# Gated product of two halves: three 64 KiB input buffers, products packed over rows already read, one store per pair of tiles

## The chip, the core and the metric

The kernel runs on one core of one Trainium2 chip. The time is the device time of one execution in microseconds (us), the median of three runs. The profile shows one execution; its span, from the first to the last instruction that it records, is a little shorter than the run's time.

Four names are needed. ACT is the engine that computes activation functions, DVE the one that multiplies tensors; SP here only issues transfers. A transfer between main memory (DRAM) and the on-chip memory (SBUF, 128 partitions) is put on the queue of SP or of ACT, and 16 DMA engines carry it out. A queue is worked off in order.

## The reference

```python
def setup_inputs():
    batch, seq, dim = (32, 512, 2048)
    return {'x': np.random.randn(batch, seq, dim).astype(np.float32)}

def reference(x):
    half_dim = x.shape[-1] // 2
    x1, x2 = (x[..., :half_dim].copy(), x[..., half_dim:].copy())
    silu_x1 = x1 * (1 / (1 + np.exp(-x1)))
    return (silu_x1 * x2).astype(np.float32)
```

The input is 16,384 rows of 2,048 float32 values (134.22 MB), the output 16,384 rows of 1,024 (67.11 MB).

## The kernel before

The rows are cut into 16 tiles of 1,024 rows. A tile puts `K = 8` rows on each of the 128 partitions: 64 KiB of input and 32 KiB of output per partition. Two tiles that follow each other form a pair (`RUN = 2`): partition p holds 16 rows that are neighbours in DRAM, the first 8 in the pair's even tile, the other 8 in its odd one. So one load reads 64 KiB at a stretch for each partition, and one store writes 32 KiB at a stretch.

There are two input buffers `xt0`, `xt1` and two output buffers `ot0`, `ot1`, used in turn.

- `load(i)` (through `move`, line 77) puts the load of tile i on SP's queue. It waits until the tile two before has been multiplied, since that frees its buffer.
- `compute(i, ...)` applies silu in place to the first half of each row on ACT (line 96), then multiplies both halves into `ot` on DVE (line 102). A tile is one ACTIVATE and one multiply. The first tile is cut in four parts of 2 rows (`FIRST`), the last in parts of 2, 3 and 3 rows (`LAST`), so that DVE can start on a part while ACT works on the next.
- `store(i, ...)` (line 77 again) puts the store of tile i on ACT's queue, where it waits for the tile's multiplies. The first tile's store is cut in three by partitions (`OPENING`), the last tile's in three by rows.
- `settle_all_but(1, ...)` makes SP wait for every transfer but the last and for the last multiplies (line 67), ahead of the wait that ends the kernel.
- `implied` tells the framework that a dependency is covered by another, so that it adds no wait for it; `after` fixes the order in which transfers take their semaphores.

The order on ACT and DVE is the order of the program (`manual_schedule`). In the loop each tile is computed, then its store and the load of the tile after next are put on their queues.

Of the kernel before, what the change touches and what calls it, by code (L numbers as in the profile page):

```python
# [1 line left out]

# [4 lines left out]


@with_exitstack
def kernel(  # L10
    ctx: ExitStack,
    tc: tile.TileContext,
    x: bass.AP,
    out: bass.AP,
):


    nc = tc.nc
    P = nc.NUM_PARTITIONS

    x_flat = x.flatten_outer_dims()
    out_flat = out.flatten_outer_dims()
    num_rows, in_cols = x_flat.shape
    half = in_cols // 2
    dt = x_flat.dtype

    K = 8
    FIRST = [2] * (K // 2)
    LAST = [2, 3, 3]
    OPENING = [  # L30
        (slice(0, None, 4), slice(None)),
        (slice(2, None, 4), slice(None)),
        (slice(1, None, 2), slice(None)),
    ]
    RUN = 2
    n_tiles = num_rows // (P * K)

    pool = ctx.enter_context(tc.tile_pool(name="pool", bufs=1))
    xts = [pool.tile([P, K, in_cols], dt, name=f"xt{b}") for b in range(2)]
    ots = [pool.tile([P, K, half], dt, name=f"ot{b}") for b in range(2)]  # L40

    def view(flat, i):
        return flat.rearrange("(g p t k) d -> g t p k d", p=P, t=RUN, k=K)[i // RUN, i % RUN]

    ctx.enter_context(tc.manual_schedule(engines={mybir.EngineType.Activation, mybir.EngineType.DVE}))

    sent = []
    loads, stores, silus, muls = {}, {}, {}, {}

    def implied(later, earlier, reason):  # L50
        for x in later:
            for y in earlier:
                tc.declare_no_dep(x, y, reason=reason)

    def earlier(done, i):
        return [ins for j in range(i % 2, i, 2) for ins in done[j]]

    def after(later, first):
        tc.add_manual_dep(
            later,  # L60
            first.name,
            mybir.DependencyInfo(mybir.DependencyClass.NoSync, mybir.DependencyReason.DATA),
            reason="order in which the transfers take their semaphores",
        )

    def settle_all_but(n, others):
        rest = nc.sync.nop(nofuse=True)
        for ins in sent[:-n] + others:
            tc.add_manual_dep(
                rest.ins,  # L70
                ins.name,
                mybir.DependencyInfo(mybir.DependencyClass.Sync, mybir.DependencyReason.DATA),
                reason="sync sees each earlier transfer land before the last ones",
            )

    def move(queue, out, in_):
        ins = queue.dma_start(out=out, in_=in_).ins  # L77
        sent.append(ins)
        return ins

    def load(i):
        loads[i] = [move(nc.sync, xts[i % 2][:], view(x_flat, i))]
        if i >= 2:
            implied(loads[i], earlier(loads, i), "the multiplies that this load awaits came after those loads")
            implied(loads[i], earlier(silus, i), "the multiplies that this load awaits came after those activations")

    def parts(sizes):
        assert sum(sizes) == K
        return [slice(sum(sizes[:n]), sum(sizes[:n + 1])) for n in range(len(sizes))]

    def compute(i, ot, chunks):
        xt = xts[i % 2]
        silus[i], muls[i] = [], []
        for ks in chunks:
            silus[i].append(
                nc.scalar.activation(  # L96
                    out=xt[:, ks, :half],
                    in_=xt[:, ks, :half],
                    func=mybir.ActivationFunctionType.Silu,
                ).ins  # L100
            )
            muls[i].append(nc.vector.tensor_mul(out=ot[:, ks], in0=xt[:, ks, :half], in1=xt[:, ks, half:]).ins)  # L102
        implied(muls[i], loads[i], "each multiply awaits an activation that came after the load")
        if i >= 2:
            implied(silus[i], earlier(silus, i), "the load that this activation awaits came after those activations")
            implied(silus[i], earlier(muls, i), "the load that this activation awaits came after those multiplies")
            implied(muls[i], earlier(muls, i), "the store that this multiply awaits came after those multiplies")

    def store(i, ot, pieces):
        ov = view(out_flat, i)  # L110
        stores[i] = [move(nc.scalar, ov[ps, ks], ot[ps, ks]) for ps, ks in pieces]

    ALL = slice(None)
    load(0)
    load(1)
    for i in range(n_tiles):
        ot = ots[i % 2]
        last = i == n_tiles - 1
        compute(i, ot, parts(FIRST if i == 0 else LAST if last else [K]))
        pieces = [(ALL, ALL)]  # L120
        if i == 0:
            pieces = OPENING
        elif last:
            pieces = [(ALL, ks) for ks in parts(LAST)]
        load_first = i // 4 % 2
        if load_first and i + 2 < n_tiles:
            load(i + 2)
        store(i, ot, pieces)
        if load_first and i + 2 < n_tiles:
            after(stores[i][0], loads[i + 2][0])  # L130
        if not load_first and i + 2 < n_tiles:
            load(i + 2)
            after(loads[i + 2][0], stores[i][-1])
    settle_all_but(1, muls[n_tiles - 1])


# [1 line left out]
_INS = ['x']  # L138
_OUTS = [((32, 512, 1024), 'float32')]


# [23 lines left out]
```

## Time and profile before

| | |
|---|---|
| median of 3 runs | 470.94 us (470.73 to 471.01) |
| span of the profiled execution | 469.19 us |
| median less span | 1.75 us |
| bytes moved, mean rate over the span | 201.33 MB, 429 GB/s |
| loads | 16, median 42.2 us from issue to landing |
| stores of a whole tile | 14, median 42.0 us from issue to landing |
| ACTIVATE of a whole tile | 7029 ns |
| multiply of a whole tile | 8692 ns |
| ACTIVATE of 2 rows, of 3 rows | 1900 ns, 2747 ns |
| multiply of 2 rows, of 3 rows | 2288 ns, 3355 ns |

The profiled execution's time beyond its span is not recorded by itself; the table's third row stands for it. "q1" in the profile is SP's queue and holds the loads, "q10" is ACT's and holds the stores. "ACT" and "DVE" rows are work of an engine, "ACTq" and "SPq" rows are transfers being put on a queue, which take no time of the engine proper. The packet records of the trace, which the prediction uses too, give each contiguous run that a DMA engine moves its start, its length and its queue. In a row, "x4" counts instructions, and the bracket gives the time that the engine sat idle before it and what ended that.

### The profile page before, as it was taken

The numbers are of one execution on the slowest core, as the hardware profiler recorded it, in microseconds if no ns is written. First come the engines' busy times: TensorE is split into PE (matmuls) and PEld (weight loads), VectorE is DVE, ScalarE is ACT, GpSimd is POOL, SyncE is SP. The second block draws the span as 40 slices with busy tenths as digits, with TensorE's granted clock in tenths as the row PEclk, the third lists the DMA queues.
The fourth block names the chain that finished last, engine by engine and source line by source line (L and its number), as shares of the span: only waits on it lengthen the run. The fifth ranks groups of instructions, "written<-read, shape, count | busy, mean of one in ns | idle before, by whom it ended". The sixth has DMA issues, their size and how long they took to land.

```text
span 469.2 us, 156 instructions
## 1 busy us (share of the span) xinstructions
DVE 139.5 (30%) x21; ACT 114.2 (24%) x22; POOL 0.2 (0%) x4
## 2 busy tenths in 40 slices
DVE  0070522407034070330704307042070520605152
ACT  1051405032050410504105050050501405014060
POOL 0000000000000000000000000000000000000000
DMA  8999999999999999999999999999999999999998
GB/s 358 447 447 374 475 402 433 416 492 402 411 439 486 408 402 447 475 419 402 444 439 458 402 436 413 492 402 416 433 486 408 402 447 475 419 402 444 450 402 358
DMA packets 4928, 201.33 MB, mean 429 GB/s; under 512 B 576, under 2 KB 576, under 8 KB 576
## 3 DMA queue, kind: packets, MB, share of 16 engines
q1 hardware_dynamic: 2304, 134.22, 66.4%
q10 hardware_dynamic: 2624, 67.11, 33.2%
HBM read 134.22 MB, written 67.11 MB: 429 GB/s over the span
## 4 chain that ended last, share of the span: by engine, by line
DMA 72%; DVE 14%; ACT 11%; DVEq 1%; issue 0%; SPq 0%
DMA xt<-in_x_dram 72%; DVE ot L102 14%; ACT xt L96 11%; DVEq L160 1%; SPq L77 0%
## 5 line engine op out<-in xcount | busy, mean ns | idle before, releaser
L102 DVE TENSOR_TENSOR ot<-xt 128x8192 f32<-128x8192 f32 (+2 forms) x21 | 139.5, 6659 | 320.8 <-ACT xt L96 320.8
L96 ACT ACTIVATE xt<-xt 128x8192 f32<-128x8192 f32 (+2 forms) x21 | 112.9, 5400 | 341.4 <-DMA xt<-in_x_dram 341.4
L96 ACT ACT_TABLE_LOAD x1 | 1.3, 1283 | 0.7 <-PEq L149 0.7
L149 POOL MEMSET const-bfloat16-1.0<- 128x1 bf16 x1 | 0.1, 102 | 0.0
L149 POOL MEMSET const-uint8-127<- 128x1 uint8 x1 | 0.1, 102 | 0.0
L149 POOL MEMSET const-float32-0.0<- 128x1 f32 x1 | 0.1, 99 | 0.2 <-issue 0.2
L149 POOL MEMSET const-float32-1.0<- 128x1 f32 x1 | 0.1, 99 | 0.0
## 6 DMA issues: line engine op xcount, KB each, us to landing
out_dram<-ot ACTq DMA_DIRECT2D x14, 4096.0 KB, 42.0
out_dram<-ot ACTq DMA_DIRECT2D x3, 1024.0 KB, 12.0
out_dram<-ot ACTq DMA_DIRECT2D x2, 1536.0 KB, 7.9
out_dram<-ot ACTq DMA_DIRECT2D x1, 2048.0 KB, 37.2
xt<-in_x_dram SPq DMA_DIRECT2D x16, 42.2
```

The lines of the kernel that those rows point to most:

```text
L96: nc.scalar.activation(out=xt[:, ks, :half], in_=xt[:, ks, :half], func=mybir.ActivationFunctionType.Silu,).ins
L102: muls[i].append(nc.vector.tensor_mul(out=ot[:, ks], in0=xt[:, ks, :half], in1=xt[:, ks, half:]).ins)
L149: nc = _bacc.Bacc("TRN2", target_bir_lowering=False, num_devices=1)
L160: with _tile.TileContext(nc) as tc:
```

## The change

Three input buffers of 64 KiB per partition take the place of two input and two output buffers: `even0` and `even1` for the even tiles of alternate pairs, and `odd` for every odd tile. There is no output buffer. The products of a pair are written into the pair's even buffer, as 16 rows of 4 KiB: those of the even tile into its first 32 KiB, over input rows that have been read, those of the odd tile into the other 32 KiB. Each pair is then stored in one transfer, 64 KiB at a stretch per partition, 8 stores in all where there were 20.

Every even tile is computed in two parts of 4 rows (`EVEN`), every odd tile in parts of 2, 3 and 3 (`ODD`). Three loads are put on SP's queue at the start. The load of the next odd tile waits for the products of the present one; the load of the even tile two pairs on waits for the store of the present pair, which reads the same buffer. The store of the last pair but one is put on ACT's queue after the two activations of tile 14 instead of at the end of its own pair; the last pair's store is a single transfer, after all of tile 15. `OPENING`, `FIRST`, `settle_all_but`, `after` and the uses of `implied` go.

```diff
     K = 8
-    FIRST = [2] * (K // 2)
-    LAST = [2, 3, 3]
-    OPENING = [
...
     RUN = 2
+    EVEN = [4, 4]
+    ODD = [2, 3, 3]
     n_tiles = num_rows // (P * K)
+    n_pairs = n_tiles // RUN
...
-    xts = [pool.tile([P, K, in_cols], dt, name=f"xt{b}") for b in range(2)]
-    ots = [pool.tile([P, K, half], dt, name=f"ot{b}") for b in range(2)]
-
-    def view(flat, i):
-        return flat.rearrange("(g p t k) d -> g t p k d", p=P, t=RUN, k=K)[i // RUN, i % RUN]
+    evens = [pool.tile([P, K * in_cols], dt, name=f"even{b}") for b in range(2)]
+    odd = pool.tile([P, K * in_cols], dt, name="odd")
+
+    x_tiles = x_flat.rearrange("(g p t k) d -> g t p (k d)", p=P, t=RUN, k=K)
+    out_pairs = out_flat.rearrange("(g p r) d -> g p (r d)", p=P, r=RUN * K)
...
+    def home(i):
+        return odd if i % 2 else evens[i // 2 % 2]
...
+    def load(i):
+        loads[i] = [move(nc.sync, home(i)[:], x_tiles[i // 2, i % 2])]
+
+    def compute(i):
+        xt = home(i)[:].rearrange("p (k d) -> p k d", k=K)
+        products = evens[i // 2 % 2][:].rearrange("p (r d) -> p r d", r=RUN * K)
         silus[i], muls[i] = [], []
-        for ks in chunks:
+        for ks in parts(ODD if i % 2 else EVEN):
             silus[i].append(
...
+            rs = slice(i % 2 * K + ks.start, i % 2 * K + ks.stop)
+            muls[i].append(
+                nc.vector.tensor_mul(out=products[:, rs], in0=xt[:, ks, :half], in1=xt[:, ks, half:]).ins
+            )
...
+    def store(g):
+        stores[g] = [move(nc.scalar, out_pairs[g], evens[g % 2][:])]
...
-    settle_all_but(1, muls[n_tiles - 1])
+    for i in range(3):
+        load(i)
+    for g in range(n_pairs):
+        last = g == n_pairs - 1
+        compute(2 * g)
+        if last:
+            store(g - 1)
+        compute(2 * g + 1)
+        if g < n_pairs - 2 or last:
+            store(g)
+        if not last:
+            load(2 * g + 3)
+        if g + 2 < n_pairs:
+            load(2 * g + 4)
```

More of the change, by code (lines that the diff above doesn't have):

```diff
@@ L27 @@
     K = 8
-    FIRST = [2] * (K // 2)
-    LAST = [2, 3, 3]
-    OPENING = [
[L31 to L34, printed above, removed]
     RUN = 2
+    EVEN = [4, 4]
+    ODD = [2, 3, 3]
     n_tiles = num_rows // (P * K)
+    n_pairs = n_tiles // RUN
     pool = ctx.enter_context(tc.tile_pool(name="pool", bufs=1))
-    xts = [pool.tile([P, K, in_cols], dt, name=f"xt{b}") for b in range(2)]
-    ots = [pool.tile([P, K, half], dt, name=f"ot{b}") for b in range(2)]
-    def view(flat, i):
-        return flat.rearrange("(g p t k) d -> g t p k d", p=P, t=RUN, k=K)[i // RUN, i % RUN]
+    evens = [pool.tile([P, K * in_cols], dt, name=f"even{b}") for b in range(2)]
+    odd = pool.tile([P, K * in_cols], dt, name="odd")
+    x_tiles = x_flat.rearrange("(g p t k) d -> g t p (k d)", p=P, t=RUN, k=K)
+    out_pairs = out_flat.rearrange("(g p r) d -> g p (r d)", p=P, r=RUN * K)
     ctx.enter_context(tc.manual_schedule(engines={mybir.EngineType.Activation, mybir.EngineType.DVE}))
@@ L53, in implied @@
                 tc.declare_no_dep(x, y, reason=reason)
[L55 to L74, printed above, removed]
     def move(queue, out, in_):
@@ L79, in move @@
         return ins
[L81 to L85, printed above, removed]
     def parts(sizes):
@@ L89, in parts @@
         return [slice(sum(sizes[:n]), sum(sizes[:n + 1])) for n in range(len(sizes))]
-    def compute(i, ot, chunks):
-        xt = xts[i % 2]
+    def load(i):
[3 more added lines that the diff above has]
+        products = evens[i // 2 % 2][:].rearrange("p (r d) -> p r d", r=RUN * K)
         silus[i], muls[i] = [], []
-        for ks in chunks:
+        for ks in parts(ODD if i % 2 else EVEN):
             silus[i].append(
@@ L101, in compute @@
             )
[L102 to L133, printed above, removed]
-    settle_all_but(1, muls[n_tiles - 1])
+            rs = slice(i % 2 * K + ks.start, i % 2 * K + ks.stop)
[18 more added lines that the diff above has]
+            load(2 * g + 4)
 _INS = ['x']
```

## The prediction

> **What bounds the kernel now.** I read the page first, for the busy shares, the DMA rows and the chain.
>
> ```profile
> DVE 139.5 (30%) x21; ACT 114.2 (24%) x22; POOL 0.2 (0%) x4
> DMA  8999999999999999999999999999999999999998
> ...
> q1 hardware_dynamic: 2304, 134.22, 66.4%
> q10 hardware_dynamic: 2624, 67.11, 33.2%
> ```
>
> Both compute engines idle for over two thirds of the span. The loads (q1) and stores (q10) together fill 66.4 + 33.2 = 99.6% of the 16 DMA engines. So the bytes are the bound, and the change can win only what is left idle: start and end.
>
> Then the busy share by stretch (columns: stretch, length, DVE, ACT, POOL, clock, DMA share, GB/s), to find where that rest lies.
>
> ```profile
> 391.00:449.00 58.00, 17.39 (x2) 14.06 (x2) 0.00 (x0) 1.00 1.00 434
> 449.00:457.70 8.70, 6.32 (x3) 7.22 (x3) 0.00 (x0) 1.00 0.98 425
> 457.70:469.20 11.50, 2.60 (x1) 0.00 (x0) 0.00 (x0) 1.00 0.85 363
> ```
>
> A pair of tiles takes 58.0 us with DMA full. After the last load lands (449.06) DMA stays full too: the row at 449.00 is 98% busy on what is left of tile 14's store while tile 15 is computed. I call such work *cover*. The change rearranges just that cover.
>
> Next, the DMA view from 402 to 413 us, in slices of 0.275 us, each packet counted where it starts.
>
> ```profile
> GB/s 2145 1430 238 0 0 0 0 0 0 1430 357 119 0 1907 1668 238 0 0 0 0 0 0 1072 715 119 0 1192 1907 715 0 0 0 0 0 0 953 834 119 0 1192
> ```
>
> Groups of about 3,800 (loads) and 1,900 (stores) alternate: while both queues hold work, each DMA engine takes one run of a load, one of a store, and so on. From the trace's packet records: a 64 KiB run takes 2.418 us, a 32 KiB run 1.213, a 12 KiB run 0.460, and starts of 64 KiB runs are 2.4145 apart. A transfer over 128 partitions is 8 runs on each engine. The engines run up to 0.64 us apart, and a transfer is seen as landed 0.36 us after its last run.
>
> Last, the end in order of time (start, length, engine):
>
> ```profile
> 435.92 0.34 ACTq L77 DMA_DIRECT2D out_dram<-ot  x1
> 449.08 4.56 ACT L96 ACTIVATE xt<-xt 128x2048 f32<-128x2048 f32 x2 [21.91 <-DMA xt<-in_x_dram]
> 451.02 2.29 DVE L102 TENSOR_TENSOR ot<-xt 128x2048 f32<-128x2048 f32 x1 [15.13 <-ACT xt L96]
> 453.35 0.34 ACTq L77 DMA_DIRECT2D out_dram<-ot  x1
> 453.55 2.75 ACT L96 ACTIVATE xt<-xt 128x3072 f32<-128x3072 f32 x1
> 453.68 6.63 DVE L102 TENSOR_TENSOR ot<-xt 128x3072 f32<-128x3072 f32 x2 [0.36 <-ACT xt L96]
> ```
>
> Two readings matter. The last tile in rows 2, 3, 3 takes 449.08 to 460.30 = 11.22 us. And the store at 453.35 is issued while the second ACTIVATE runs (to 453.64) and before the third starts: an issue on ACT's queue does not wait for activations that are running or ready ahead of it. One that still waits for its data does hold the queue: a semaphore check for tile 3's store, long satisfied, is recorded at 101.09, just after that tile's ACTIVATE starts at 101.08.
>
> **The change, part by part.** *Packets.* Loads stay 128 runs of 64 KiB per engine. Stores were 120 runs of 32 KiB, 8 of 8 and 16 of 12 per engine: 120 x 1.213 + 8 x 0.309 + 16 x 0.460 = 155.4 us. They become 64 of 64 KiB; priced like a load's 2.418, 154.8. With the start-to-start figure and fewer completion packets I get -0.35 (bounds -0.7 and 0).
>
> *Start.* Three loads are queued at once, and the first store waits for tile 1, not tile 0. Load 1 lands at 22.66 + 8 x 2.4145 = 41.98, its products are done 11.22 later, at 53.2, with load 2 under way since 40.96. DMA is never without work: 0. The one-off 0.85 us by which a load's runs grow just before the first store's (starts 36.14 to 39.57 in before) moves along: 0.
>
> *Middle.* Load 4 and each later even one now waits for the store two pairs back to land, and stands in SP's queue; the odd load before it is issued already. Stores take every second slot. Store 0 is issued 12.3 us, or 5.1 runs, after load 2's first run. Before, the first store was issued at 33.53, during a load's run; one more load run went, then the store's. So here: 7 runs of load 2, then alternating. When store 0's 8th run ends, 2 runs of load 3 are left, 4.83 us. Load 4 needs 0.64 + 0.36 to see the landing and 1.0 from issue to first run (load 0: 0.73 to 1.73), in all 2.0. 2.8 us to spare, and each pair repeats this, since every phase hangs on the load ahead. The added waits on SP (0.02 to 0.05 us each) hide in it. Price 0. ACT's queue holds store g behind tile 2g+1's products; tile 2g+2's load lands 11 us later, so no activation is late. In-place products: DVE and ACT off the path except for tile 15, same 11.22.
>
> *End.* No store runs while load 14 finishes alone. Store 6 stands behind tile 14's two activations; the first waits for load 14, the second is ready behind it. By the 453.35 row the store is issued as soon as the first starts, 1.0 us after load 14's last run on the earliest engine, and ready 1.0 later, inside load 15's first run. One more load run follows, then they alternate. After load 15's 8th run, store 6 has had 6 runs; 2 remain, 4.83 us of cover. The last store's first run comes 1.0 (landing) + 0.02 + 11.22 (tile 15) + 0.03 + 1.0 (issue) = 13.27 us after load 15's end. DMA then idles 13.27 - 4.83 = **8.44 us**. One run later or earlier at the join gives 6.0 or 10.9.
>
> After that pause the first run may be longer: the only row of a run on idle engines is the first of the execution, 3.225 against 2.418, +0.8 for a load. No such growth shows on a store: +0.4, bounds 0 and 0.8. The last store is one piece, so its bytes no longer flow while the tile is computed; that is in the 8.44. Without the wait gathered on SP ahead of the end (15.69 us long in its record at 449.07, hidden), some checks may follow the last landing: +0.1, bounds 0 and 0.4.
>
> Sum: -0.35 + 8.44 + 0.4 + 0.1 = +8.6 us. On the profiled span of 469.19 that is 477.8; the median 470.94 is 1.75 more, for what lies around the span, so **479.5 us**.
>
> **A rule against a row.** The Trainium skill, "DMA: Bandwidth & Descriptors", section on queues, rings and completion order, says an engine drains a whole packet, typically 9 to 17 descriptors, from one ring before it takes the next. The view from 402 us shows the switch after every single run, so here the trace differs. The rule is rival 4's.
>
> **Rivals.**
> 1. *Not slower: store 6 is really held back.* If its issue comes after both activations have run (7029 ns for a whole tile by the page, so some 7.2 us for the two), it joins after load 15's 5th run, 5 runs of cover remain (12.07), idle is 1.2, and the time is 470.94 - 0.35 + 1.2 + 0.5 = 472.3; one run later it is nil, and the time 470.7 (without a pause, no first-run cost). It decides from an issue 6 us or more after load 14 lands. For it: the order written down. Against: the 453.35 row.
> 2. *Not held at all.* If the issue passes an activation that waits, store 6 goes at tile 13's end, is gone before load 15 lands, and nothing covers: +13.27, so 470.94 - 0.35 + 13.27 + 0.5 = 484.4. Against: the check at 101.09. The Trainium skill, "Perfetto Trace Analysis", on DVE and Act instructions, has the wait in a queue of the engine while the sequencer goes on; that would give this rival, and the 101.09 record speaks against it.
> 3. *The store's run is cut.* If 64 KiB goes as two of 32, store g has 16 slots, load 2g+3 ends with 7 still to go, and load 2g+4 starts 2.0 us late, six times; at the end 10 short runs (12.1) cover all but 1.2: 470.94 + 12 + 1.2 + 0.5 = 484.6. Against: loads of the same contiguous shape are single runs, 2048 packets of 64 KiB.
> 4. *Whole transfers alternate.* Then load 15 ends before store 6 starts, whose 19.3 us cover the 13.27: 470.94 - 0.35 + 0.1 = 470.7.
>
> **How the numbers follow.** Forecast 0.82: join as worked out 0.55, one run later (477.1) 0.2, one earlier (481.9) 0.07. Rivals: 0.07, 0.05, 0.03, 0.03. The lowest of the one-later case without its 0.5 is 476.6; the one-earlier case gives 482.0 rounded up. That range holds 0.82. A difference of 0.2% is 0.94 us, about what a measurement here can tell from none. Within it: rival 4 and half of rival 1, 0.06. Faster by more: no case, since only -0.35 is to be had; 0.02 for 64 KiB store runs faster than any row shows (6% would be needed even to undo the pause). Slower: the rest, 0.92.
>
> **What would show it.** Right: stores landing in about 39 us each, the last in about 20; DMA near 1.00 until some 4.8 us after the last load, then a hole of 8 us in its row; the held store issued within 0.2 us of tile 14's first ACTIVATE; last ACTIVATE group starting near 444. Wrong: that store issued 7 us after it (rival 1) or before it (2); holes all along (3); loads landing in 20 us beside a store (4).

## The result, and the profile after

The changed kernel takes 489.29 us (median of 5 runs, 487.93 to 490.69) against 470.94 us: a ratio of 1.039, 95% interval 1.037 to 1.041. The forecast was 479.5 us, range 476.6 to 482.0. The direction was right; the loss is twice as large: 18.35 us where 8.6 were worked out. The profiled execution has a span of 487.41 us (before: 469.19).

The page of the changed kernel, the same rows as before:

```profile
DVE 142.2 (29%) x40; ACT 116.0 (24%) x41; POOL 0.2 (0%) x4
DMA  8999899999999999999999999999999999999277
...
q1 hardware_dynamic: 2304, 134.22, 65.2%
q10 hardware_dynamic: 1152, 67.11, 31.8%
...
out_dram<-even ACTq DMA_DIRECT2D x8, 43.6
```

The compute engines have not changed their part. The DMA engines fill 97.0% of the span where they filled 99.6%, and the row ends in 2 7 7: the hole that the forecast saw. But 65.2% of 487.4 is 318 us of loads, against 66.4% of 469.2, or 312 us, for the same 128 runs per engine. So the loads themselves took longer, and that was not in the sum. A store lands 43.6 us after its issue (median); the forecast had about 39.

The busy share by stretch (stretch, length, DVE, ACT, POOL, clock, DMA share, GB/s):

```profile
352.00:410.00 58.00, 17.65 (x5) 14.34 (x5) 0.00 (x0) 1.00 0.98 421
410.00:454.40 44.40, 8.97 (x3) 7.12 (x2) 0.00 (x0) 1.00 1.00 431
...
456.60:466.60 10.00, 8.85 (x3) 5.20 (x2) 0.00 (x0) 1.00 0.00 0
466.60:487.40 20.80, 0.00 (x0) 0.00 (x0) 0.00 (x0) 1.00 0.93 403
```

The third row is the hole: 10 us without a byte while DVE and ACT work on tile 15. The first row is the surprise: 58 us in mid-run at a DMA share of 0.98 move 421 GB/s, where 58 us of before moved 434. A share near 1 with a lower rate means that runs are on the engines for longer.

The end in order of time (start, length, engine):

```profile
410.15 0.33 SPq L55 DMA_DIRECT2D odd<-in_x_dram  x1
418.20 3.62 ACT L72 ACTIVATE even<-even 128x4096 f32<-128x4096 f32 x1 [12.08 <-DMA even<-in_x_dram]
418.21 0.34 ACTq L55 DMA_DIRECT2D out_dram<-even  x1
...
454.59 7.22 ACT L72 ACTIVATE odd<-odd 128x2048 f32<-128x2048 f32 x3 [29.27 <-DMA odd<-in_x_dram]
456.53 2.29 DVE L80 TENSOR_TENSOR even<-odd 128x2048 f32<-128x2048 f32 x1 [25.73 <-ACT odd L72]
459.18 6.63 DVE L80 TENSOR_TENSOR even<-odd 128x3072 f32<-128x3072 f32 x2 [0.36 <-ACT odd L72]
465.84 0.34 ACTq L55 DMA_DIRECT2D out_dram<-even  x1
```

The held store goes out at 418.21, 0.01 us after tile 14's first activation starts and while it runs to 421.82. Tile 15 takes 454.59 to 465.81 = 11.22 us, and the last store follows at once.

And who holds up SP's queue (engine, for whom: us in total, times, longest):

```profile
SPq L55 <- DMA out_dram<-even: 260.9, 6, 44.3
SPq L55 <- DVE even L80: 78.9, 7, 11.3
```

Six even loads wait for a store to land. Before, 14 loads waited for DVE and none for a store:

```profile
SPq L77 <- DVE ot L102: 400.0, 14, 31.9
```

**Where the 18 us went.** From the packet records, as a mean over the 16 DMA engines (longer runs are counted over 2.418, 1.213, 0.460 and 0.309 us, by size):

| us per engine | before | after | difference |
|---|---|---|---|
| longer load runs | 1.67 | 8.08 | +6.4 |
| engines idle up to 440 us | 0.00 | 0.69 | +0.7 |
| engines idle after 440 us (the hole) | 0.02 | 11.50 | +11.5 |
| all other busy time | 465.22 | 464.48 | -0.7 |

The rows add up to 17.9 us. The other 0.3 of the 18.2 between the two spans are small differences at the start, at the end and in how far runs overlap. The forecast had 8.4 for the hole, 0 for the first two rows.

### The profile page after: what moved, and what is told of

Its sections match the earlier page's. It is cut to its first block, busy times and chain, and to the rows that moved or that the text cites. A ratio compares the mean times of both kernels' runs of the same rounds, so it can differ in the third digit from the quotient of the medians.

```text
span 487.4 us, 195 instructions
## 1 busy us (share of the span) xinstructions
DVE 142.2 (29%) x40; ACT 116.0 (24%) x41; POOL 0.2 (0%) x4
## 3 DMA queue, kind: packets, MB, share of 16 engines
q1 hardware_dynamic: 2304, 134.22, 65.2%
## 4 chain that ended last, share of the span: by engine, by line
DMA 77%; DVE 10%; ACT 7%; DVEq 1%; issue 1%; SPq 0%; ACTq 0%
DMA odd<-in_x_dram 77%; DVE even L80 10%; ACT odd L72 7%; DVEq L125 1%; SPq L55 0%; ACTq L72 0%
## 5 line engine op out<-in xcount | busy, mean ns | idle before, releaser
L80 DVE TENSOR_TENSOR even<-odd 128x3072 f32<-128x3072 f32 (+1 forms) x24 | 71.4, 3001 | 178.9 <-ACT odd L72 178.9
L80 DVE TENSOR_TENSOR even<-even 128x4096 f32<-128x4096 f32 x16 | 70.8, 4426 | 144.7 <-ACT even L72 143.9
L72 ACT ACTIVATE odd<-odd 128x3072 f32<-128x3072 f32 (+1 forms) x24 | 57.7, 2467 | 204.4 <-DMA odd<-in_x_dram 204.4
L72 ACT ACTIVATE even<-even 128x4096 f32<-128x4096 f32 x16 | 57.0, 3608 | 140.7 <-DMA even<-in_x_dram 140.7
## 6 DMA issues: line engine op xcount, KB each, us to landing
out_dram<-even ACTq DMA_DIRECT2D x8, 43.6
```

The source lines that it names most:

```text
L72: nc.scalar.activation(out=xt[:, ks, :half], in_=xt[:, ks, :half], func=mybir.ActivationFunctionType.Silu,).ins
L80: nc.vector.tensor_mul(out=products[:, rs], in0=xt[:, ks, :half], in1=xt[:, ks, half:]).ins
```

## The experiments

Three questions were open. Is the hole what was taken for it? What makes load runs longer? And does packing in place have a part in it? Times before are 470.91, 471.03 and 470.98 us in the three groups of runs below.

**The hold undone** (`e1_no_hold`):

```diff
-        if last:
-            store(g - 1)
         compute(2 * g + 1)
-        if g < n_pairs - 2 or last:
-            store(g)
+        store(g)
```

> The changed kernel (489.3 us) with the last store but one issued at the end of its own pair instead of after tile 14's activations. Theory (the hole before the last store is what no store covers while tile 15 is computed): the held store lends one or two runs of 2.4 us of cover, so without the hold the hole grows from some 11 to some 13.5 us and the time to 491 to 493 us. Rival (the hold does nothing, since the issue passes a waiting activation): within 1 us of 489.3 and the same hole.

Measured: 493.51 us (491.86 to 494.26), ratio to before 1.0476 (1.0456 to 1.0496). That is half a microsecond above the range of the theory, and far from the rival. The engines idle 13.9 us at the end, 2.4 more than with the hold: one run. Of the other 2.6 us between the two profiled spans (492.37 and 487.41), 1.6 are longer load runs (9.71 in all) and 1.0 engines that idle earlier. The hold does hold, and is worth one run of cover.

**The last pair in pieces** (`e2_tail_pieces`; `piece(g, rows)` stores those rows of a pair):

```diff
         if last:
             store(g - 1)
+            piece(g, slice(0, K))
         compute(2 * g + 1)
-        if g < n_pairs - 2 or last:
+        if last:
+            for ks in parts(ODD):
+                piece(g, slice(K + ks.start, K + ks.stop))
+        if g < n_pairs - 2:
             store(g)
```

> The changed kernel with the last pair stored in four pieces, each as soon as its products are there (8 rows of tile 14, then 2, 3 and 3 rows of tile 15), the hold kept. Theory: the hole of some 11 us goes, and the load runs that grow beside each store's start (6.4 us per DMA engine) stay: 477 to 480 us. Rival (the longer load runs only come with the hole, or in its place): 471 to 473 us.

Measured: 480.59 us (475.55 to 482.46), ratio 1.0189 (1.013 to 1.0248). That is 0.6 us above the theory's range, and 7.6 above the rival's. The hole is gone: less than 0.2 us idle after 440 us in place of 11.50. The longer load runs are not: 9.79 us in the profiled run, with 1.9 us of engines idle before 440 us. So the two losses are separate, and the second is about 10 us by itself.

**Each tile's products stored when they are ready** (`e3_halves`):

```diff
         compute(2 * g)
-        if last:
-            store(g - 1)
+        piece(g, slice(0, K))
         compute(2 * g + 1)
-        if g < n_pairs - 2 or last:
-            store(g)
+        for ks in parts(ODD) if last else [slice(0, K)]:
+            piece(g, slice(K + ks.start, K + ks.stop))
```

> The changed kernel with every pair stored in two transfers of 32 KiB runs, each as soon as its tile is done, the last tile in three pieces, no hold. The store queue then never runs empty from tile 0 on. Theory A (a load run grows when a store comes to an empty store queue): growth at one place alone, no hole, 470.5 to 473 us. Rival C (growth comes with the in-place buffers or the engines' order, not with the queue's state): growth of about 6 us stays, 476 to 479 us.

Measured: 472.17 us (471.58 to 472.38), ratio 1.0025 (1.0014 to 1.0035). The three 64 KiB buffers and the packing in place are all still there, and nearly all of the loss is gone. The busy share by stretch, six pairs in mid-run:

```profile
57.86:405.86 348.00, 106.63 (x30) 86.03 (x30) 0.00 (x0) 1.00 1.00 434
```

The odd loads, one for each pair, show the period (the first two and the last of seven):

```profile
57.86 0.33 SPq L55 DMA_DIRECT2D odd<-in_x_dram  x1
...
115.87 0.33 SPq L55 DMA_DIRECT2D odd<-in_x_dram  x1
...
405.86 0.33 SPq L55 DMA_DIRECT2D odd<-in_x_dram  x1
```

Six pairs take 348.00 us, 58.00 each, as before the change. The same rows of the changed kernel:

```profile
53.11 0.33 SPq L55 DMA_DIRECT2D odd<-in_x_dram  x1
...
112.36 0.33 SPq L55 DMA_DIRECT2D odd<-in_x_dram  x1
...
350.05 0.33 SPq L55 DMA_DIRECT2D odd<-in_x_dram  x1
...
410.15 0.33 SPq L55 DMA_DIRECT2D odd<-in_x_dram  x1
```

357.04 us for six, 59.5 each: 9.0 us lost between 53 and 410 us. In-place packing is cleared; what differs is when the queues have work, and the length of the store's runs. No load comes late here, and the longer load runs, 2.13 us in all, stand at the start of the execution and at the first store's start alone.

**The pair's store in two transfers at the old place** (`e4_halves_together`):

```diff
     def store(g):
-        stores[g] = [move(nc.scalar, out_pairs[g], evens[g % 2][:])]
+        for rows in (slice(0, K), slice(K, RUN * K)):
+            span = slice(rows.start * half, rows.stop * half)
+            move(nc.scalar, out_pairs[g][:, span], evens[g % 2][:, span])
```

> The changed kernel with each pair's store cut in two transfers of 32 KiB runs, issued one after the other at the same place, hold kept. Theory A (empty store queue): the load runs beside each store's start still grow, 3 to 7 us in all, and the load of the even tile, which waits for both, comes some 2 us late six times: 488 to 502 us. Rival D (it is the 64 KiB length of the store's runs that makes load runs grow): growth falls below 2 us per engine in the profile.

Measured: 481.61 us (479.6 to 484.66), ratio 1.0249 (1.0216 to 1.0283). Neither expectation came true as stated, and the edit did not do what its name says. The first half depends only on the even tile, so its issue passed the running activations: 41.93 us, when tile 1's first activation starts, not 53. That also covers the end, and there is no hole. Loads still grew by 5.56 us and stores by 2.40 with 32 KiB store runs, so the 64 KiB store run is not the cause. The growth has a pattern: after load 4 (issued at 101.29, engines idle 0.15 to 1.2 us ahead of it), load 8 and load 12 it is 1.8 us per engine each time (store runs by 0.76, load runs by 1.08 at load 4), and next to nothing at loads 6, 10 and 14, which were in time.

**The stream by itself.** Theory A, that a store queue which starts from empty costs up to 1.5 us, was then tried without any compute: two load buffers, a constant stored, loads that wait only for the load two before; `look(i)` is an ACTIVATE of 8 values, which runs when load i has landed.

```python
for i in range(n_tiles):
    look(i)
    for s in GATES.get(i, []):
        store(s)
    if i + 2 < n_tiles:
        load(i + 2)
...
GATES = {0: [(g, 0, 1) for g in range(n_pairs)]}
...
GATES = {2 * g: [(g, 0, 1)] for g in range(n_pairs)}
...
GATES = {i: [(i // 2, i % 2, 2)] + ([(7, 1, 2)] if i == 14 else []) for i in range(n_tiles - 1)}
```

The three lines at the end belong to `m1_stores_at_once`, `m8_stores_apart` and `m15_half_stores_apart`; `store((g, h, step))` stores partitions h, h + step and so on of pair g.

> A stream by itself: the same 16 loads of 64 KiB runs and 8 stores of 64 KiB runs, with no silu, no products and a constant stored in their place; each load waits only for the one two before it to land, and all 8 stores are put on their queue when load 0 lands, so that the store queue starts from empty once. Theory A (a queue that starts from empty beside the other costs up to 1.5 us on each DMA engine): one growth of about 0.9 us, 469 to 471 us. Rival (growth comes with compute and the in-place buffers): none, 468 to 469.5 us.

> The same stream, with store g put on its queue when load 2g lands, so that the store queue runs empty and starts again 8 times, with no load issued late. Theory A: 8 starts of 0.05 to 1.5 us, 3 to 8 us of growth per engine, 472 to 479 us. Rivals (growth comes with compute, with late loads or with the hole): as the stream that starts once, within 1 us.

> The same stream and bytes, with 16 stores over every second partition (4 runs of 64 KiB per engine each), one put on its queue as each load lands (the last two together), so 15 starts from empty. Theory A, if each start costs the same: twice the growth of the stream with 8, 476 to 488 us. Rival (the cost goes with the bytes or the run length, not with the number of starts): as the stream with 8.

Measured: 475.23 us (474.13 to 476.78), 477.69 us (477.01 to 477.93) and 498.54 us (498.29 to 499.71). By the times alone, the second would pass for theory A. Its packet records say otherwise: the first store's start costs 0.87 us per engine, the other seven 0.02 to 0.22. **Theory A is wrong.** The time is long because three of the 16 engines end at 470.3 to 474.1 and the other 13 by 467.7: a transfer is over when its last engine is. The first stream has the same trait (one engine ends at 473.5, three at 470.3 to 470.7, the mean at 469.0). It also has 0.8 us of longer load runs that theory A did not foresee, at a load that came late:

```profile
98.72 2.74 SPq L44 DMA_DIRECT2D xt<-in_x_dram  x2
```

The first of these two is load 3. It was issued when load 2 had landed, and the engines moved one or two more store runs in its place. The trait and this growth are the likely reason that 469 to 471 was missed. The third has 19.9 us of longer load runs and 4.6 of store runs. Most of it is in the load runs between a store's own four runs, not in the run ahead of its start, and in the first half no load came late. A store over every second partition does something else, what is open, and nothing follows from it about starts.

**Before, with its loads cut in two** (`e5_before_cut_loads`):

```diff
-        loads[i] = [move(nc.sync, xts[i % 2][:], view(x_flat, i))]
+        loads[i] = [
+            move(nc.sync, xts[i % 2][:, ks], view(x_flat, i)[:, ks]) for ks in (slice(0, K // 2), slice(K // 2, K))
+        ]
```

> The kernel before with each load cut into two transfers of 32 KiB runs (4 rows per partition each), nothing else. Loads and stores then have runs of one length, as in the changed kernel, so a tile's store is done in 8 x 2.42 = 19.4 of the 29 us of a tile and the store queue runs empty once a tile, though buffers, products and stores are those of before. Theory A: growth beside about 15 starts, 475 to 487 us. Rival (the 64 KiB store runs, the packing or the late loads are the cause): 470.5 to 472 us.

Measured: 475.08 us (474.78 to 475.33), ratio 1.0086 (1.0071 to 1.0101): the number that theory A asked for, and again for another reason. Load runs are 1.64 us longer in all, as in before. The store queue runs empty in every tile and starts again without cost. What is lost is a hole of 3.1 us at the end: with runs of one length the store of tile 14 ends 3.6 us after the last load in place of 9.3, and no longer covers tile 15. This is the hole's mechanism once more, in the kernel before.

**Idle engines, forced** (`m8_idle`: the second stream, with three loads that also wait for a store). In the kernels so far most growth in mid-run came where a load had been released too late. So theory E: after engines have had nothing to do, the next run on each queue is longer.

```diff
-        nc.sync.dma_start(out=xts[i % 2][:], in_=x_tiles[i // 2, i % 2])
+        ins = nc.sync.dma_start(out=xts[i % 2][:], in_=x_tiles[i // 2, i % 2]).ins
+        if i in (4, 8, 12):
+            tc.add_manual_dep(
+                ins,
+                stored[-1].name,
...
```

> The stream with 8 stores apart (no silu, no products, a constant stored), with one edit: loads 4, 8 and 12 also wait for the store before them to land, so that three times both queues are empty and every DMA engine idles for some 1.5 us. Theory A (start from an empty store queue) has fallen: that stream started its store queue from empty 8 times and grew only at the first. Theory E (after a DMA engine has had nothing in either queue, the next load's first run grows by some 0.8 us and the load run ahead of the next store by some 1.0 to 1.5): 3 x (1.5 idle + 0.8 + 1.2) = 10.5 us more than that stream's 477.7, so 487 to 490 us, and growth at those three places alone. Rival F (an idle engine costs its idle time only): 3 x 1.5 = 4.5 us more, 481 to 483 us, and no growth.

Measured: 487.57 us (487.07 to 488.07), 9.9 us over the stream without the waits; theory E had 10.5, its rival 4.5. That the time fits theory E so well is luck: there were six pauses, not three, and the mean engine ends 15.6 us later (at 484.0 in place of 468.3). The time rose by less, as three slow engines had set the end of the stream without the waits. The packet records can tell more. The busy share of both, from 53 us to the last store's issue (first without, then with the waits):

```profile
53.00:435.00 382.00, 0.00 (x0) 2.71 (x13) 0.00 (x0) 1.00 1.00 433
```

```profile
53.00:446.00 393.00, 0.00 (x0) 2.71 (x13) 0.00 (x0) 1.00 0.98 416
```

The engines idled at six places, not three (the loads behind the late ones came late too): 7.8 us on a mean engine. Growth rose with it from 2.8 to 10.7 us, nearly all of it in the first runs after a pause: 0.55 to 0.64 us where only a load started again (121, 242 and 363 us), 0.76 to 0.80 on the store and 1.10 to 1.21 on the load where both did (163, 284 and 404 us). No silu and no product is computed here. A late load costs the engines' idle time and about as much again.

Theory E blames the pause, and the waits that forced the pauses made the loads late too. Three places in the packet records tell the two apart, and speak for the late load:

- The last store of the changed kernel starts after 11.5 us of idle engines, and its first run is only 0.04 us longer. No load is in play there.
- Load 3 of the first stream came late beside a store queue that never ran empty. One of the 16 engines paused, yet the first two runs of the load were longer on all 16, by 0.77 us on a mean engine.
- At load 12 of the changed kernel 9 engines paused, and the first run was longer on all 16.

So the growth goes with loads that are not yet queued when an engine is ready for them. What lengthens the runs then is not shown. It isn't the whole of it either: the first store's start brings 0.86 us in the kernel before and 0.97 in the changed one, with no late load and no pause just ahead of it, and the third stream has growth beside loads in time.

**The late loads removed from the changed kernel.** Loads in 32 KiB runs let a store through sooner, so even loads are released in time. The edit, on the kernel with pieces and on the changed kernel itself:

```diff
-        loads[i] = [move(nc.sync, home(i)[:], x_tiles[i // 2, i % 2])]
+        loads[i] = []
+        for n in range(2):
+            span = slice(n * K // 2 * in_cols, (n + 1) * K // 2 * in_cols)
+            loads[i].append(move(nc.sync, home(i)[:, span], x_tiles[i // 2, i % 2][:, span]))
```

> The changed kernel with the last pair stored in pieces (480.6 us), and each load cut into two transfers of 32 KiB runs. A store then gets every second slot beside runs of half the length and lands some 10 us earlier, so that no even load is released late, while the store queue runs empty for longer than before. Theory E (idle engines, through even loads released late, bring the growth): growth at the first store alone, no gaps in mid-run, 471 to 474 us. Theory A (growth at each start from an empty store queue) or in-place buffers: 478 to 482 us.

> The changed kernel (489.3 us) with the same cut of the loads and nothing else; its last store is still one piece. Theory E: the 6.4 us of growth and 0.8 us of gaps go, the hole before the last store stays and grows to 13 to 14 us, as the held store is done before the last load lands: 483 to 486 us. Theory A: 488 to 492 us.

Measured: 486.32 us (484.45 to 487.12) and 492.59 us (491.06 to 495.1); both expectations of the time were missed, the second also by theory A, 0.6 us above its range. The part that concerns late loads came true. In `e7_cut_loads` idle time before 440 us falls from 0.69 to 0.15 us, and the stores that the changed kernel started at a cost of 1.03 and 1.49 us (pairs 3 and 4) start at 0.16 and 0.10. But another growth took its place: 4.54 us on loads and 3.85 on stores. More than half of it stands between 350 and 390 us, behind the start of one store; in `e6_pieces_cut_loads` it is spread over mid-run. The hole at the end is 13.3 us in `e7_cut_loads`, as expected, and one of 7.4 us opens in `e6_pieces_cut_loads`. What makes runs grow in this other way is not settled.

**All pairs side by side.** For each even load of the changed kernel, `e1_no_hold` and `e2_tail_pieces`: the idle time and growth at that load's start, and the growth at the next store's start, as means over the 16 engines.

| | pairs | cost at the load's start, us | at the next store's start, us |
|---|---|---|---|
| load came late | 10 | 0.43 to 1.28 | 0.93 to 1.49 |
| load in time | 8 | 0.00 to 0.13 | 0.07 to 0.27 in seven, 1.08 in one |

In the DMA view of the changed kernel, in slices of 0.275 us, the two kinds can be seen. From 111 us, behind a load in time, groups start about 2.4 us apart:

```profile
GB/s 0 0 0 0 2383 1192 238 0 0 0 0 0 0 2383 1430 0 0 0 0 0 0 477 1907 953 477 0 0 0 0 0 1430 1192 715 477 0 0 0 0 0 1430
```

From 229 us, behind a late one, the group at 232.0 (slice 12) is followed by one at 235.05 to 235.6 (slices 23 to 25), some 3.3 us later, on nearly every engine:

```profile
GB/s 0 0 1430 1668 238 238 238 0 0 0 0 1430 1668 238 238 238 0 0 0 0 0 0 238 1192 1430 238 238 0 238 238 0 477 1430 953 238 238 238 0 238 0
```

Why all 16 engines pay at the store's start when, as here, only 11 of them had paid at the load's is open.

No version that beats the kernel before came out of this. The best one, with each tile's products stored when they are ready, is 1.26 us slower.

## Why the prediction was right or wrong

**Right: the direction, and half of its mechanism.** Nothing could be won from the bytes: -0.7 us of other busy time, at the lower bound. The hole before the last store is there, and pieces remove it.

**Right about the held store's issue, one run off at its join.** The held store was issued with tile 14's first activation (418.21), so rival 1, a hold through both activations, is out. It also had all its products since 410.12 and did not pass the activation that waited for load 14, so rival 2 is out, and with it the rule of the Trainium skill's "Perfetto Trace Analysis" as the prediction read it for this order of an activation and a transfer. Tile 15's 11.22 us, and last landing to last issue, are as worked out. The store queue takes every second slot, so rival 4 is out; its runs are 1024 of 64 KiB, so rival 3 is out. On 12 of the 16 engines the store joined behind three runs of load 15, not two, so that three of its own were left for cover. This is the forecast's case of one run later, with 477.1 us; it should have made the hole smaller.

**Mis-sized: the hole.** 8.44 us were forecast, 11.50 measured, by three errors that partly cancel.

- The sum had "1.0 (landing)". In the packet records the slowest engine ends its last run of load 15 at 451.75, and the word that reports it goes out only at 454.16, behind one more store run; tile 15 starts at 454.59. The landing so takes 2.84 us, and from load end to the last store's first run (466.75, mean) it is 15.0 us in place of 13.27: +1.7.
- The cover was 4.83 us, two runs. With the later join the mean engine had 6.6 us of store left when its own load ended: -1.8.
- The cover was counted from a common end of load 15. The engines start their last run of it between 444.71 and 449.33, 4.6 us apart, and the slowest ends 3.2 us after the mean. The mean engine is through with the held store at 455.2, only 3.5 us after the slowest has its load: +3.2.

That the first two nearly cancel is luck. The last store's first run was priced at +0.4 us for the pause before it; it measured 0.04.

**Wrong: "Middle. Price 0."** This is the step that failed; it cost some 7 of the 9.8 us that are missing. The even loads do not hide behind the odd ones, and a late load costs more than its lateness. Three errors stand behind it.

First, "0.64 + 0.36 to see the landing". The word that reports a transfer takes a turn of its own: in both traces it follows the store's last run by one whole load run, 2.41 us, as long as loads are queued beside it. Load 1 of the kernel before shows the same: its last run ends at 43.79, its word comes 1.21 us later, behind a 32 KiB store run. The 0.36 holds for load 0, which has no store beside it. Before, nobody waited for a store's word in mid-run; after, six loads do. Part of this error cancels: the even load's own word takes a turn too, the store gains a slot by it, and three runs of the odd load are left at its end in place of two. So it was in pair 0, where load 4 was issued at 96.24 and came in time. In pairs 2 and 4 the store joined later on 8 and 10 engines, two runs were left there, and the 2.8 us to spare become 0.4.

Second, engines taken to be at most 0.64 us apart, and a first run 1.0 us after the issue. A load waits for the word of the slowest engine. From pair 1 on that word came 1.3 to 2.0 us after the mean, and the fastest engine was through with the odd load 0.4 to 0.8 us ahead of the mean. Where engines stood waiting, first runs came 1.0 to 3.3 us after the load's issue: load 12 was issued at 335.28, and its last engine began at 338.57.

Third, from the part on the start, "the one-off 0.85 us [...] moves along: 0". It was taken for a price of the first store alone. Growth of that size comes back where even loads are released late: three times in the profiled run, with 2.3 us at the loads, idle time included, and 3.7 at the stores that follow. As late loads also push the engines further apart, the next ones come late more easily, which fits the spread of 487.9 to 490.7 us where before had 0.3.

**What the sign rested on.** The forecast put nearly all of "slower" on the hole. Either loss alone gives the sign: without the hole (`e2_tail_pieces`) the kernel is still 9.7 us slower than before (480.59 against 470.91), and the hole alone is 11.5 us in the profiled run.

## What to carry to other kernels

When a kernel is bound by its transfers, a wait that ties a load to a store's landing is on the path even if the sum shows a few microseconds to spare: count the turn that the completion itself takes, the distance between the engines and the time from issue to first run on the last of them, before calling it free. Look too at how run lengths match the bytes of two queues that share the DMA engines run by run. Here loads have twice the bytes, and twice the run length kept both queues full at all times. With runs of one length the store queue ran empty: in mid-run that alone cost nothing (`e5_before_cut_loads`), but the cover at the end shrank. Fewer and larger stores gave up the balance and the cover, for 0.7 us of packet time.

## What the runs showed of the hardware that was not expected

- A transfer's completion word waits for its own turn: 2.41 us behind a 64 KiB load run in both kernels, 1.21 us behind a 32 KiB store run in the kernel before, and no time where the other queue is empty.
- Around a load that comes late, runs are longer: by 0.2 to 0.7 us on the mean engine at the load itself, and by 0.9 to 2.0 us around the next store's start. A store queue that starts beside loads in time costs 0.02 to 0.22 us (seven starts of the second stream), and a store that starts after 11.5 us of idle engines, with no load beside it, 0.04 us.
- From a load's issue to its first run on an engine that stands waiting took 1.0 to 3.3 us (loads 8, 10 and 12 of the changed kernel).
- A DMA share near 1 is no proof of full rate: the changed kernel from 53.11 to 410.15 us and `e3_halves` from 57.86 to 405.86 us, six pairs each, both show 1.00, the one with 425 GB/s, the other with 434:

```profile
53.11:410.15 357.04, 106.62 (x30) 86.03 (x30) 0.00 (x0) 1.00 1.00 425
```

- Engines that start 0.7 us apart can end 7 us apart (467.0 to 474.1 us in the second stream), and a transfer is as late as its last engine.
